# Norm gains on x instead of on w_in and wq, in a two-layer decoder trunk

## The chip, the core and the metric

The kernel runs on one core of one Trainium2 chip. The metric is the device time of one execution in microseconds: the median of several runs. A hardware profile of one such execution shows each instruction of the engines: PE (TensorE, matrix products; its weight loads, PEld, are shown apart), DVE (VectorE), ACT (ScalarE), POOL (GpSimd) and SP, which here issues the loads of weights.

## What is computed

Two layers act on 256 tokens of width 1024, in float32. Each sub-layer normalizes its input first:

```
def rms_norm(x, gain):
    y = x32 * lax.rsqrt(jnp.mean(x32 * x32, axis=-1, keepdims=True) + EPS)
    return (y * gain.astype(jnp.float32)).astype(x.dtype)
...
for l in range(DEPTH):
    h = h + 0.5 * swiglu(rms_norm(h, ffn1_norm[l]), ...)
    h = h + hybrid_mixer(rms_norm(h, mix_norm[l]), w_in[l], ...)
    h = h + memory_cross_attention(rms_norm(h, xattn_norm[l]),
                                   rms_norm(mem, mem_norm[l]), wq, wkv, wo)
    h = h + 0.5 * swiglu(rms_norm(h, ffn2_norm[l]), ...)
return rms_norm(h, final_norm)
```

The mixer multiplies by one matrix `w_in` (1024 x 2048), whose columns give the input of a state-space model and q, k and v of a differential attention. The cross attention's queries are `rms_norm(h) @ wq` (1024 x 1024). A gain has one number per input column, that is, per row of the weight matrix: `(x * gain) @ w` is the same as `x @ (gain * w)`. The factor `rsqrt(...)` is one number per token and is multiplied into the product afterwards.

## The kernel before

**Three products for one.** Operands are split into a high part in the fast float32 format (fp32r) and a low part, the remainder. A product is the sum of three: high x high, high x low, low x high. ACT makes the high part (a copy, `whi` for weights, `xh` for x), DVE the low one (source minus high part, `wlo`, `xl`). Weights move through the array as the streamed operand, 512 columns at a time; x, transposed, is the loaded one.

**Units.** All weights come in an order made out beforehand (`stream_plan`, L112) as 414 units of 128 x 1024, each loaded by one 512 KB DMA from SP's queue into one of four raw buffers. An entry of the plan holds the name, the layer, the number, a kind, the gain and a skew. Kind A (gate and up weights, `w_in`, `wkv`, `wq`) has two row groups of 128 with 512 columns each, kind B one row group with 1024. Kind S belongs to a scheme of seven products instead of eight in the second-form ffns. Skew 4 marks units of which four are used in a row by the first token tile and then again by the second: the first chunk behind a seam and the units of `blocks`. Skew 1 marks the rest. `chunk` (L140) enters the four units that give 512 output columns.

**Splitting.** A unit is split either in halves or whole. `split_unit` (L606) does one half of 512 columns: where the plan names a gain, ACT copies with it as scale and DVE does `raw * gain - high` as one SCALAR_TENSOR_TENSOR; otherwise it is a plain copy and a subtraction. `split_whole` (L549) does all 1024 columns with one instruction on each engine, without a gain. `feed` (L527) decides when: it goes along the plan, a few planner microseconds ahead of the matmuls, and splits whole where the entry is of an ffn and has no gain, or is of kind S. `tick` calls it before each half unit's matmuls; these wait for the end of the split they read.

**Where gains sit.** In the first ffn of layer 0, in `w_in`, `wkv`, `wq` and `w_out` they are multiplied into the weights. For `ffn2` and for `ffn1` of layer 1 they are multiplied into x: `prep` (L799) adds a sub-layer's output to the residual `h`, transposes it on PE in two halves of four 128 x 128 blocks, and calls `split_gain` (L494) or the plain `split` (L490) on each half. `split_gain` uses four ACT copies and four DVE instructions of 128 columns, one for each block, as each block has its own column of gains; the plain one uses one of 512 on each engine. `prep` runs once per token tile at the start of each sub-layer, then starts the sum of squares for `rstd`.

**Order of work.** Everything is put into a fixed order by a planner inside the program: a clock (`Clock`) adds up modelled costs of each instruction, and tasks (generators) for evacuations, attention and the state-space model are resumed when their modelled time comes. So what an instruction is modelled to cost sets where other instructions are put in each engine's queue.

**Around the change.** `mixer` (L1380) makes four chunks of `w_in`, three of `wkv`, then `w_glu` and `w_out`; `cross` makes two chunks of `wq`, one of `wkv`, then `wo`. `project` (L678) runs one chunk into two PSUM tiles `mm`, one for each tile of 128 tokens. There are two such buffers, so that the evacuation of a chunk (`z`, an ACT copy with `rstd` as scale) must be done before the next chunk's matmuls for that tile. The first chunk of a sub-layer runs all of token tile 0, then all of tile 1. In the trace the tile names tell the stage: `mm<-whi,xh` are products of x, `mm<-whi,mem` those of the memory (`wkv`), `acc<-whi,gT` the ffns' down products, `acc<-whi,yT` those of `w_glu`. Most instructions carry the line of a helper: L369 the matmuls, L380 the transposes, L330 ACT, L293 DVE.

Of the kernel before, what the change touches and what calls it, by code (L numbers as in the profile page):

```python
# [76 lines left out]
def second_items(nm):  # L77

    seen = {}
    for item in (SECOND if nm == "ffn2" else SECOND_ONE).split():  # L80
        k = seen[item] = seen.get(item, -1) + 1
        yield item[0], int(item[1:]), k
# [29 lines left out]
def stream_plan():  # L112

    plan = []
    for l in range(L):
        def ffn(nm):
            for j in range(NCH):
                for kp in range(4):
                    plan.append((nm + "_gu", l, 4 * j + kp, "A", (nm, l, 2 * kp), 4 if j == 0 and len(plan) >= 4 else 1))
                if j >= LAG:  # L120
                    for f in range(2):
                        plan.append((nm + "_dn", l, 2 * (j - LAG) + f, "B", None, 1))
            for n in range(2 * (NCH - LAG), 2 * NCH):
                plan.append((nm + "_dn", l, n, "B", None, 2 * LAG))

        def second(nm):
            for kind, j, k in second_items(nm):
                if kind == "P":
                    plan.append((nm + "_gu", l, 4 * j + k, "A", None, 4 if j == 0 else 1))
                elif kind == "D":  # L130
                    plan.append((nm + "_dn", l, 2 * j + k, "B", None, 1))
                else:
                    _, loads, operand, add = PAIR[k]
                    for u in range(2):
                        n = [4 * (j + a) + 2 * b + u for _, a, b in loads]
                        plan.append((nm + "_gu", l, n, "S", ((nm, l, j), u, [x[0] for x in loads], operand, add), 1))
            for n in range(2 * (NCH - LAG), 2 * NCH):
                plan.append((nm + "_dn", l, n, "B", None, 2 * LAG))

        def chunk(nm, c, norm, skew):  # L140
            for kp in range(4):
                plan.append((nm, l, 4 * c + kp, "A", (norm, l, 2 * kp), skew))

        ffn("ffn1") if l == 0 else second("ffn1")
        for c in range(4):
            chunk("w_in", c, "mix", 4 if c == 0 else 1)
        for c in range(3):
            chunk("wkv", c, "mem", 1)
        for k in range(4):
            plan.append(("w_glu", l, k, "B", None, 4))  # L150
        for k in (4, 5, 6, 7, 0, 1, 2, 3):
            plan.append(("w_out", l, k, "B", ("ssm", l, k) if k < 4 else ("sub", l, 0), 4))
        for c in range(2):
            chunk("wq", c, "xattn", 4 if c == 0 else 1)
        chunk("wkv", 3, "mem", 1)
        for k in range(8):
            plan.append(("wo", l, k, "B", None, 4))
        second("ffn2")
    need, at, i = [], 0.0, 0
    while i < len(plan):  # L160
        n = plan[i][5]
        need += [at + STEP * k for k in range(n)]
        at += STEP if plan[i][3] == "S" else 2 * STEP * n
        i += n
    ahead, at, stage = [], 0, None
    for nm, l, n, kind, _, skew in plan:
        at = at + 1 if (nm[:4], l) == stage else 0
        stage = nm[:4], l
        long = nm[:3] == "ffn" and at >= 16 and skew == 1 or nm == "w_in" and at >= 4 or nm == "wkv" and n < 8
        ahead.append(LEAD_LONG if long else LEAD)  # L170
    return plan, need, ahead
# [213 lines left out]
class Trunk:  # L385
    def __init__(self, ctx, tc, io):
# [19 lines left out]
        self.tp = P("tp", 1, space=bass.MemoryType.PSUM)  # L406
        self.dram = P("dram", 1, space=bass.MemoryType.DRAM)
        self.plan, self.need, self.ahead = stream_plan()
        self.main = 0.0
        self.upos = self.nload = self.nsplit = self.nfree = 0  # L410
# [116 lines left out]
    def feed(self, least=-1):  # L527

        c = self.c
        prev, c.cur = c.cur, self.stream  # L530
        n = len(self.plan)
        while self.nsplit < 2 * n:
            u, q = divmod(self.nsplit, 2)
            if u >= self.nfree + N_W or (u > least and self.need[u] + q * STEP / 2 > self.main + self.ahead[u]):
                break
            self.split_next(self.plan[u][0].startswith("ffn") and self.plan[u][4] is None or self.plan[u][3] == "S")
        c.cur = prev

    def split_next(self, whole=False):
# [259 lines left out]
    def prep(self, t, acc, coef, gain=None):  # L799
        h = self.h[t]  # L800
        t0 = []
        for n in range(2):
            s = slice(512 * n, 512 * n + 512)
            self.v.scalar_tensor_tensor(h[:, s], acc[n], coef, h[:, s], op0=ALU.mult, op1=ALU.add)
            t0.append(self.c.cur.t)
        self.acc_done()
        x = self.xt()
        for n in range(2):
            self.c.cur.t = t0[n]
            yield  # L810
            yield from self.tp_wait()
            p = self.transpose4(h, [512 * n + 128 * i for i in range(4)])
            if gain is not None:
                self.split_gain(x, n, p, *gain)
            else:
                o = [a[:, 4 * n:4 * n + 4, :].rearrange("p a b -> p (a b)") for a in x]
                self.split(o[0], o[1], p)
            self.tp_done(p)
        self.x[t] = x
        with self.c.aside():  # L820
            self.row_stat(t)
# [1083 lines left out]
    def run(self):  # L1905
        c = self.c
        self.setup()
        preps = None
        prep = lambda coef, gain=None: (lambda t, acc: self.prep(t, acc, coef, gain))
        z, tb = {}, {}  # L1910
        small = c.spawn(self.ssm_small(z), START[0])
        tables = self.tables(0, z, tb, small)
        c.spawn(self.chain(self.setup_mem(0), self.setup_mem(1), self.setup_bias(), self.setup_lam()), START[1])
        for l in range(L):
            if l == 0:
                preps = self.ffn("ffn1", preps, prep(0.5))
            else:
                tb, tables = {}, []
                preps = self.ffn_second("ffn1", preps, prep(0.5), lambda: tables.extend(self.tables(l, z, tb, None)))
            preps = self.mixer(l, preps, tb, tables, prep(1.0))  # L1920
            preps = self.cross(l, preps, prep(1.0, ("ffn2", l)))
            if l == L - 1:
                self.fn = self.s4t([128, 1024], name="fn")
                self.g.dma_start(self.fn, self.io["final_norm"].to_broadcast([128, 1024]))
            preps = self.ffn_second("ffn2", preps, prep(0.5, ("ffn1", l + 1)) if l < L - 1 else (lambda t, acc: self.final(t, acc, 0.5)))
        c.wait(*preps)
        c.drain()
        assert self.upos == len(self.plan) == self.nfree
# [9 lines left out]
def lay_out(a):  # L1938
# [11 lines left out]
    for l in range(L):  # L1950
# [9 lines left out]
        groups["w_glu", l] = type_b(f["ssm_w_glu"][l])  # L1960
        groups["w_out", l] = type_b(f["w_out"][l])
    wst = np.concatenate([groups[s, l][i:i + 1] for s, l, n, _, _, _ in stream_plan()[0] for i in (n if isinstance(n, list) else [n])], axis=0)
    col = lambda v: v.reshape(-1, 128).T
    gains = np.concatenate(
# [31 lines left out]
```

## Time and profile before

| | us |
|---|---|
| median of 3 runs (1193.57 to 1193.97) | 1193.92 |
| the profiled execution | 1193.89 |
| its span, first to last instruction | 1192.1 |
| DMA traffic read, MB | 207.00 |

The page of the profile gives the busy time of each engine, its share of the span, and the longest groups of instructions. In such a group `whi<-raw,gains 128x512 ... x280 | 184.0, 714 | 10.6` means: written tile, read tiles, shape, count, busy us, mean ns of one, and idle us of the engine just ahead of them with what ended it. In the timeline a row has the start, the length, the engine and the instruction; equal neighbours are merged and counted. Matmuls overlap on PE, so the time that one costs is the distance between two starts, not its length. Idle time of an engine is put down to what it waited for.

The first mixer's products begin at about 208 us of the span and its `w_in` part ends at about 262 us; its cross attention begins at about 346 us, the second ffn of layer 0 at 418 us. Layer 1's mixer begins at about 794 us, its cross attention at 933 us.

### The profile page before, as it was taken

The numbers are of one execution on the slowest core, as the hardware profiler recorded it, in microseconds if no ns is written. First come the engines' busy times: TensorE is split into PE (matmuls) and PEld (weight loads), VectorE is DVE, ScalarE is ACT, GpSimd is POOL, SyncE is SP. The second block draws the span as 40 slices with busy tenths as digits, with TensorE's granted clock in tenths as the row PEclk, the third lists the DMA queues.
The fourth block names the chain that finished last, engine by engine and source line by source line (L and its number), as shares of the span: only waits on it lengthen the run. The fifth ranks groups of instructions, "written<-read, shape, count | busy, mean of one in ns | idle before, by whom it ended". The sixth has DMA issues, their size and how long they took to land.

```text
span 1192.1 us, 17474 instructions
## 1 busy us (share of the span) xinstructions
PE 1182.4 (99%) x6571; PEld 967.8 (81%) x6571; DVE 909.7 (76%) x1331; ACT 707.1 (59%) x1141; POOL 46.7 (4%) x104
## 2 busy tenths in 40 slices
PE   9999999999999999999999999999999999999997
PEld 7888788877888888888888887888778888888886
DVE  5799676598767688889588985766978575888885
ACT  6665554656866566565466644455767665656553
POOL 1200001000100000000000000010001000000000
PEclk9999999999999999999999999999999999999999
DMA  8656545644544465474557364556436445836542
GB/s 276 227 185 208 156 165 170 195 126 140 177 160 141 159 229 213 142 263 126 176 199 266 123 199 150 176 154 180 150 101 208 150 149 176 305 120 240 183 125 87
DMA packets 59973, 210.90 MB, mean 177 GB/s; under 512 B 7168, under 2 KB 8288, under 8 KB 59888
## 3 DMA queue, kind: packets, MB, share of 16 engines
q1 hardware_dynamic: 56304, 202.92, 52.1%
q0 software_dynamic: 2000, 5.24, 1.6%
q10 hardware_dynamic: 1584, 1.62, 0.6%
q8 instruction: 51, 0.84, 0.3%
q14 instruction: 34, 0.28, 0.1%
HBM read 207.00 MB, written 1.05 MB: 175 GB/s over the span
## 4 chain that ended last, share of the span: by engine, by line
PE 97%; ACT 1%; issue 0%; DMA 0%; DVE 0%; POOLq 0%; POOL 0%; ACTq 0%; DVEq 0%
PE mm L369 50%; PE acc L369 33%; PE tp L369 10%; PE tp L380 5%; DMA gains<-in_gains 0%; ACT junk L330 0%; ACT whi L330 0%; DVE h L293 0%; DVE ang L293 0%; ACT on L330 0%; ACT z L330 0%; DVE wlo L293 0%; POOLq L1992 0%; ACT xh L330 0%; POOL rstd L353 0%
## 5 line engine op out<-in xcount | busy, mean ns | idle before, releaser
L369 PE MATMUL mm<-whi,xh 128*128 128x512 f32 x736 | 295.3, 401 | 1.1 <-ACT whi L330 1.0
L293 DVE TENSOR_TENSOR wlo<-raw,whi 128x1024 fp32r<-128x1024 f32 (+1 forms) x228 | 248.0, 1108 | 51.8 <-ACT whi L330 51.1
L369 PE MATMUL mm<-whi,xl 128*128 128x512 f32 x736 | 287.5, 391 | 0.0
L369 PE MATMUL mm<-wlo,xh 128*128 128x512 f32 x736 | 286.9, 390 | 0.3 <-DVE wlo L293 0.3
L330 ACT ACTIVATE whi<-raw 128x1024 fp32r<-128x1024 f32 (+1 forms) x228 | 214.0, 967 | 54.6 <-PE acc L369 25.6
L293 DVE SCALAR_TENSOR_TENSOR wlo<-raw,gains,whi 128x512 fp32r<-128x512 f32 x280 | 198.7, 746 | 53.0 <-ACT whi L330 50.9
L369 PE MATMUL acc<-whi,gT 128*128 128x512 f32 (+1 forms) x704 | 235.3, 395 | 0.0
L330 ACT ACTIVATE whi<-raw,gains 128x512 fp32r<-128x512 f32 x280 | 184.0, 714 | 10.6 <-PE mm L369 4.6
L369 PEld LDWEIGHTS mm<-whi,xh 128*128 128x128 f32 x736 | 138.2, 188 | 31.7 <-ACT whi L330 1.6
L369 PEld LDWEIGHTS mm<-whi,xl 128*128 128x128 f32 x736 | 138.1, 188 | 29.6 <-DVE xl L293 0.3
L369 PEld LDWEIGHTS mm<-wlo,xh 128*128 128x128 f32 x736 | 138.5, 188 | 26.5 <-DVE wlo L293 1.0
L369 PEld LDWEIGHTS acc<-whi,gT 128*128 128x128 f32 x704 | 132.0, 188 | 26.5
L369 PE MATMUL acc<-wlo,gT 128*128 128x512 f32 (+1 forms) x352 | 136.8, 389 | 0.0
L369 PE MATMUL mm<-whi,mem 128*128 128x512 f32 x256 | 92.4, 409 | 0.2
L330 ACT ACTIVATE z<-mm,rstd 128x256 f32<-128x256 f32 (+1 forms) x70 | 37.8, 547 | 71.7 <-PE mm L369 71.1
L369 PEld LDWEIGHTS acc<-wlo,gT 128*128 128x128 f32 x352 | 66.3, 188 | 12.1
L330 ACT ACTIVATE gT<-tp 128x512 fp32r<-128x512 f32 x44 | 26.4, 599 | 60.4 <-PE tp L380 60.3
L369 PEld LDWEIGHTS mm<-whi,mem 128*128 128x128 f32 x256 | 48.1, 188 | 12.7 <-ACT z L330 1.6
L293 DVE TENSOR_TENSOR wlo<-blkX,whi 128x1024 fp32r<-128x1024 f32 x40 | 48.6, 1220 | 9.9 <-ACT whi L330 9.9
L330 ACT ACTIVATE whi<-blkX 128x1024 fp32r<-128x1024 f32 x40 | 42.0, 1055 | 19.5 <-PE mm L369 7.0
L369 PE MATMUL mm<-wlo,mem 128*128 128x512 f32 x128 | 50.2, 393 | 0.0
L293 DVE TENSOR_TENSOR gT<-tp,gT 128x512 fp32r<-128x512 f32 x44 | 30.3, 688 | 24.6 <-ACT gT L330 24.6
(261 smaller groups left out, 1583.4 us busy)
## 6 DMA issues: line engine op xcount, KB each, us to landing
raw<-in_wst SPq DMA_DIRECT2D x342, 512.0 KB, 4.1
blkX<-in_wst SPq DMA_DIRECT2D x10, 512.0 KB, 4.6
blkP<-in_wst SPq DMA_DIRECT2D x10, 512.0 KB, 7.9
blkY<-in_wst SPq DMA_DIRECT2D x10, 512.0 KB, 9.0
blkQ<-in_wst SPq DMA_DIRECT2D x10, 512.0 KB, 9.6
raw<-in_wst SPq DMA_DIRECT2D x4, 256.0 KB, 5.7
mem<-in_mem POOLq DMA_DIRECT2D x2, 512.0 KB, 4.3
uq<-z ACTq DMA_DIRECT2D x8, 128.0 KB, 5.8
```

Source lines behind the costliest of these rows:

```text
L293: r = getattr(self.e, name)(*a, **k)
L330: r = self.e.activation(out, in_, func, **k)
L369: r = self.e.matmul(out, lhsT, rhs, **k)
L380: r = self.e.transpose(out, in_, ident)
```

## The change

Four places of the code differ. The entries of `w_in` and `wq` in the plan lose their gain. The `prep` in front of the mixer and of the cross attention gets it instead, so that these call `split_gain` on x. The test in `feed` now asks for `ffn`, `w_in` or `wq`, without a gain, and for skew 1. Units of the ffns with skew 4 are thereby split in halves too. The number of matmuls, transposes and loads stays as it is.

```
         def chunk(nm, c, norm, skew):
             for kp in range(4):
-                plan.append((nm, l, 4 * c + kp, "A", (norm, l, 2 * kp), skew))
+                plan.append((nm, l, 4 * c + kp, "A", norm and (norm, l, 2 * kp), skew))
...
         for c in range(4):
-            chunk("w_in", c, "mix", 4 if c == 0 else 1)
+            chunk("w_in", c, None, 4 if c == 0 else 1)
...
         for c in range(2):
-            chunk("wq", c, "xattn", 4 if c == 0 else 1)
+            chunk("wq", c, None, 4 if c == 0 else 1)
...
-            self.split_next(self.plan[u][0].startswith("ffn") and self.plan[u][4] is None or self.plan[u][3] == "S")
+            self.split_next(self.plan[u][0][:3] in ("ffn", "w_i", "wq") and self.plan[u][4] is None and self.plan[u][5] == 1 or self.plan[u][3] == "S")
...
             if l == 0:
-                preps = self.ffn("ffn1", preps, prep(0.5))
+                preps = self.ffn("ffn1", preps, prep(0.5, ("mix", l)))
             else:
                 tb, tables = {}, []
-                preps = self.ffn_second("ffn1", preps, prep(0.5), lambda: tables.extend(self.tables(l, z, tb, None)))
-            preps = self.mixer(l, preps, tb, tables, prep(1.0))
+                preps = self.ffn_second("ffn1", preps, prep(0.5, ("mix", l)), lambda: tables.extend(self.tables(l, z, tb, None)))
+            preps = self.mixer(l, preps, tb, tables, prep(1.0, ("xattn", l)))
```

## The prediction

> **What bounds the kernel now.** I read the page first: the span, the busy shares, and the chain that ended last.
>
> ```profile
> span 1192.1 us, 17474 instructions
> ...
> PE 1182.4 (99%) x6571; PEld 967.8 (81%) x6571; DVE 909.7 (76%) x1331; ACT 707.1 (59%) x1141; POOL 46.7 (4%) x104
> ...
> PE 97%; ACT 1%; issue 0%; DMA 0%; DVE 0%; POOLq 0%; POOL 0%; ACTq 0%; DVEq 0%
> ```
>
> The tensor engine covers 99% of the span and 97% of the chain. Busy does not prove that it is at its peak, since its matmuls overlap: one of 512 columns lasts about 0.39 us here, and a wait shorter than that hides inside "busy". So the second view is the chain of waits in order of time, for the rate of a stretch without a break.
>
> ```profile
> 50.34 10.88 PE mm L369 x48
> ```
>
> 48 matmuls in 10.88 us are 0.227 us from one to the next. That is the floor, and the change adds or removes no matmul and no transpose: only time that the engine loses above this floor can move the end. The third view, the engine's timeline, shows such losses. I looked for places where the next matmul starts later than 0.227 us, and for those that only a wait explains. In the first layer's mixer and at the seams around it the plain ones are these (two matmuls merged into one row last 0.61 us when nothing holds them):
>
> ```profile
> 250.21 0.51 PE L369 MATMUL mm<-whi,xh 128*128 128x512 f32 x1
> 250.55 0.40 PE L369 MATMUL mm<-wlo,xh 128*128 128x512 f32 x1
> ...
> 297.32 0.97 PE L369 MATMUL mm<-whi,mem 128*128 128x512 f32 x2
> ...
> 315.00 0.61 PE L369 MATMUL acc<-whi,yT 128*128 128x512 f32 x2
> 315.62 0.50 PE L369 MATMUL acc<-wlo,yT 128*128 128x512 f32 x1
> 315.96 0.63 PE L369 MATMUL acc<-whi,yT 128*128 128x512 f32 x2
> ...
> 728.68 0.39 PE L369 MATMUL acc<-whi,gT 128*128 128x512 f32 x1
> 729.18 0.50 PE L369 MATMUL mm<-whi,xh 128*128 128x512 f32 x1
> ...
> 883.70 0.97 PE L369 MATMUL mm<-whi,mem 128*128 128x512 f32 x2
> ```
>
> At 250.21 the next start comes 0.34 us later, 0.11 too much. At 297.32 the pair takes 0.97 instead of 0.61, so 0.36. At 315.00 two starts take 0.62 instead of 0.45, and the one behind them 0.34, so 0.17 + 0.11. Together 0.75 us in a layer; the second layer repeats them (883.70 is the twin of 297.32), so 1.5 us, and the hole at 728.68, 0.50 - 0.23 = 0.27, makes 1.8 us. **All that the mixers can give back is about 1.8 us of 1192.1, or 0.15%.** A measurement of this kernel can tell about 0.2% (2.4 us) from no change.
>
> **The change part by part.** The weights' copies, and the weight loads, are grouped in the view of instructions by line and shape (busy us, mean ns after the count):
>
> ```profile
> L293 DVE TENSOR_TENSOR wlo<-raw,whi 128x1024 fp32r<-128x1024 f32 x180 | 217.1, 1220 | 38.1 <-ACT whi L330 37.7
> L293 DVE SCALAR_TENSOR_TENSOR wlo<-raw,gains,whi 128x512 fp32r<-128x512 f32 x280 | 198.7, 746 | 53.0 <-ACT whi L330 50.9
> L330 ACT ACTIVATE whi<-raw 128x1024 fp32r<-128x1024 f32 x180 | 186.6, 1057 | 44.5 <-PE acc L369 15.5 <-DMA raw<-in_wst 10.3 <-PE mm L369 7.0
> L330 ACT ACTIVATE whi<-raw,gains 128x512 fp32r<-128x512 f32 x280 | 184.0, 714 | 10.6 <-PE mm L369 4.6 <-issue 2.6 <-DVE wlo L293 1.3
> ...
> L369 PEld LDWEIGHTS mm<-whi,xh 128*128 128x128 f32 x736 | 138.2, 188 | 31.7 <-ACT whi L330 1.6 <-issue 1.3 <-DVE z L293 0.9
> ...
> L293 DVE TENSOR_TENSOR wlo<-raw,whi 128x512 fp32r<-128x512 f32 x48 | 30.9, 687 | 13.7 <-ACT whi L330 13.4
> ...
> L330 ACT ACTIVATE whi<-raw 128x512 fp32r<-128x512 f32 x48 | 27.4, 632 | 10.2 <-PE acc L369 10.2
> ...
> L293 DVE TENSOR_TENSOR xl<-tp,xh 128x512 fp32r<-128x512 f32 x28 | 19.3, 689 | 20.9 <-ACT xh L330 20.9
> ...
> L330 ACT ACTIVATE xh<-tp 128x512 fp32r<-128x512 f32 x28 | 16.7, 597 | 47.2 <-PE tp L380 47.2
> ...
> L330 ACT ACTIVATE xh<-tp,gains 128x128 fp32r<-128x128 f32 x48 | 13.6, 368 | 25.3 <-PE tp L380 25.3
> L293 DVE SCALAR_TENSOR_TENSOR xl<-tp,gains,xh 128x128 fp32r<-128x128 f32 x48 | 13.5, 345 | 5.3 <-ACT xh L330 5.3
> ```
>
> Neighbours on an engine overlap, so I price by busy over count: with a gain and 512 columns 0.657 (ACT) and 0.710 us (DVE); without, 0.571 and 0.644; whole units of 1024, 1.037 and 1.206; for x, a plain 512 costs 0.597 and 0.689, four gained 128s cost 4 x 0.283 = 1.13 and 4 x 0.281 = 1.12.
>
> Removed: w_in has 16 units a layer and wq 8, so 48 units or 96 gained halves: ACT -63.1, DVE -68.2 us. In their place come 32 whole units (those with skew 1): +33.2 and +38.6; and 16 units in plain halves (the first chunk of each, skew 4): +18.3 and +20.6. The streams so get lighter by 11.6 us (ACT) and 9.0 (DVE).
>
> Added: at four stage starts, two token tiles of two halves each, 16 plain copies of x become 64 gained ones: +8.6 on ACT, +7.0 on DVE. And the new condition asks for skew 1 of the ffn units too: the first chunk and the last four down units of the three second-form ffns and the last four of the first ffn, 28 units, fall back from whole to halves: 56 x 0.571 - 28 x 1.037 = +2.9 on ACT, +2.3 on DVE.
>
> **Net: -0.1 us on ACT and +0.3 on DVE.** The change saves next to no engine time; it moves about 10 us per engine from the streams to stage starts and seams. So the question is only whether the matmuls notice at either place.
>
> The streams: a first half of a whole unit now waits until 1024 columns are split. The tightest w_in half before:
>
> ```profile
> 222.66 4.07 DVE L293 SCALAR_TENSOR_TENSOR wlo<-raw,gains,whi 128x512 fp32r<-128x512 f32 x6 [1.84 <-ACT whi L330]
> ```
> ```profile
> 226.01 0.39 PE L369 MATMUL mm<-wlo,xh 128*128 128x512 f32 x1
> ```
>
> The first of these six copies, done about 223.41, is read by the matmul at 226.01: 2.6 us early. A whole unit delays a first half by at most one half copy, 0.6 us, and its second half comes no later. No hole; the cover is that lead. The loads behind it, on SP's queue, start when the raw buffer is released, with the second half as now; queue and sizes stay.
>
> The starts: behind the transposes of the residual, PE's queue needs x, and ACT's and DVE's queues hold the first chunk's weights behind it. Without gains (first mixer) and with them (second ffn) this looks so:
>
> ```profile
> 203.48 0.60 ACT L330 ACTIVATE xh<-tp 128x512 fp32r<-128x512 f32 x1 [6.06 <-PE tp L380]
> 203.97 0.71 ACT L330 ACTIVATE whi<-raw,gains 128x512 fp32r<-128x512 f32 x1
> ```
> ```profile
> 413.88 2.27 ACT L330 ACTIVATE xh<-tp,gains 128x128 fp32r<-128x128 f32 x8 [6.18 <-PE tp L380]
> 416.02 1.07 ACT L330 ACTIVATE junk<-h 128x1024 bf16<-128x1024 f32 x1
> ```
> ```profile
> 210.75 1.40 DVE L293 SCALAR_TENSOR_TENSOR wlo<-raw,gains,whi 128x512 fp32r<-128x512 f32 x2
> ```
> ```profile
> 212.62 0.39 PE L369 MATMUL mm<-wlo,xh 128*128 128x512 f32 x1
> ```
>
> One plain half occupies ACT 0.49 us (203.48 to 203.97), so two 0.98; eight gained copies 2.14 (413.88 to 416.02): +1.16 us per tile ahead of the weights. The tightest weight behind the first tile is the first of the two at 210.75: done about 211.49, read at 212.62, 1.1 us early. From 1.16 I take back what the lighter halves give, 0.09 on ACT (0.657 - 0.571) and 6 x 0.066 on DVE (0.710 - 0.644): net 0.7 later, 0.4 us left. If the give-back fails, 0.05 is missing and the matmul behind it costs 0.11 more: 0.16 at each of four starts, 0.6 us. The second tile's x has a precedent, the ffn's start:
>
> ```profile
> 423.46 2.25 DVE L293 SCALAR_TENSOR_TENSOR xl<-tp,gains,xh 128x128 fp32r<-128x128 f32 x8 [0.60 <-ACT xh L330]
> ```
> ```profile
> 424.36 0.40 PE L369 MATMUL mm<-whi,xl 128*128 128x512 f32 x1
> ```
>
> The first low part is there at 423.81 (0.345 after its start), 0.55 before its matmul, and nothing stops. The sum of squares, and with it POOL's rstd, comes the same 1.16 later for each tile; the evacuations that need it stand behind 24 matmuls (5.4 us). Cost zero, upper end 0.6. The ffn's own start now gets half units, of which the first is ready sooner: zero.
>
> What no row shows is how the planner, whose modelled costs change, regroups the small-matrix bursts among the matmuls:
>
> ```profile
> 233.29 0.69 PE mm L369 x3
> ...
> 235.06 0.89 PE mm L369 x3
> ```
>
> Three matmuls take 0.89 us behind a burst of small matrices and 0.69 otherwise. A burst split off or merged is worth 0.2 us; five either way, my estimate from some twenty such groups in a mixer, make 1.0 us. I take zero, the row as it stands.
>
> Sum: 0 on the profiled execution, whose own time is 1193.89 us (span 1192.1, the rest around it), beside a median of 1193.92. **Forecast 1193.9 us**, with its own range 1192.9 to 1195.5 (1.0 of bursts down; 1.0 and 0.6 of starts up).
>
> **The rivals.**
> (1) Faster: the lighter streams close the holes. 1193.9 - 1.8 = 1192.1; with five bursts merged 1191.1. For it: the hole at 315.00 waits for a low part made late by a full DVE. Against it: it lies in w_glu, far behind w_in, and nothing there gets lighter.
>
> (2) Slower: evacuation behind wide copies. A chunk has two PSUM tiles, and the next chunk's first matmuls write into them, so ACT must evacuate between:
>
> ```profile
> 247.76 0.71 ACT L330 ACTIVATE whi<-raw,gains 128x512 fp32r<-128x512 f32 x1
> ...
> 249.47 0.68 ACT L330 ACTIVATE z<-mm,rstd 128x512 f32<-128x512 f32 x1
> ```
>
> The second evacuation ends at 250.15 and the matmul at 250.21 has waited for it. If a whole copy (1057 ns, not 714) stands in front, it is 0.34 later, plus the 0.11 behind every hole: 0.45. There are four such boundaries per layer in the mixer and two in the cross attention, 12 in all: 5.4 us at most, 2.7 if half are hit, so 1196.6. It decides from the point where a whole copy starts inside the last 0.34 us before an evacuation that has no slack. Against it: here ACT sits idle for 0.50 us between the two, waiting for a transpose, which would swallow the 0.34.
> The Trainium skill speaks for this one ("Perfetto Trace Analysis", Optimizing Scalar/DVE Operations): larger operations help where the engine is saturated, and where it isn't but causes bubbles elsewhere, breaking instructions up may help. By that rule whole units are the wrong way at 59% of ACT; the trace shows one place in reach and decides nothing yet.
>
> (3) PE only looks full, matmuls hide waits for DVE throughout, and lighter streams shorten them by all that DVE is relieved of there: 1193.9 - 9.0 = 1184.9. Against it, the unbroken 0.227 us. The skill's rule ("Perfetto Trace Analysis", Identifying the Most-Contended Engine) is to judge PE by its weight loads' busy share, not by matmuls'; by it the 81% would leave room. Trace: a load lasts 0.188 us of each 0.227, 83%, in stretches without any wait, so 81% is nearly its ceiling here.
>
> (4) The planner puts the copies at the old times and the relief becomes idle time on ACT and DVE: the forecast's time.
>
> **How the numbers follow.** Forecast with (4) 0.70, (1) 0.15, (2) 0.13, (3) 0.02. Faster by over 0.2% (below 1191.5): a quarter of (1) and all of (3), 0.06. Slower by over 0.2% (above 1196.3): two thirds of (2), 0.09. Same: 0.85. The range runs from 1191.9, just past the 1.8 us of holes, to 1196.0, past the forecast's upper end and into (2); it leaves out about 0.15.
>
> **What would show it.** Counts: 184 whole plain weight splits, 136 plain halves, 184 gained ones, 112 gained copies of x. ACT's and DVE's busy sums within about 2 us of 707.1 and 909.7. PE's gaps at 297, 315 and 729 unchanged; a w_in chunk's matmuls free of new holes. Rival (2) would show as later first matmuls of chunks with an evacuation just ended; a start that fails, as a late second matmul in the fourth unit of a first chunk. I am wrong if the span moves by more than 2.4 us, or if the busy sums do not balance.

## The result and the profile after

The changed kernel takes 1216.03 us (median of 5 runs, 1215.08 to 1217.04) beside 1193.92 for the one before (1193.52 to 1194.18) on the same chip: a ratio of 1.0185, 95% interval 1.0174 to 1.0197. That is 22.1 us slower, and outside the range that the prediction gave. Its page has these lines:

```profile
span 1214.2 us, 17567 instructions
...
PE 1188.4 (98%) x6571; PEld 973.1 (80%) x6571; DVE 910.6 (75%) x1375; ACT 708.8 (58%) x1187; POOL 45.4 (4%) x104
...
PEclk9999999999899999999999999999989999999999
...
PE 94%; ACT 3%; DMA 1%; issue 1%; DVE 1%; ACTq 0%; POOLq 0%; POOL 0%; DVEq 0%
```

ACT and DVE do what was forecast: 708.8 and 910.6 us, 1.7 and 0.9 more than before. The number of PE's instructions is the same. Yet PE's share of the chain fell from 97% to 94%, and in two of the 40 slices, one in each layer, the granted clock is below nine tenths. So PE waits somewhere, although ACT and DVE have hardly more to do.

To see where, I cut the span at events that both kernels have: the transposes of `h` with which the mixers, the cross attentions and the second ffn begin. The view of windows gives for each stretch its length, the busy time of PE, PEld, DVE, ACT and POOL, the granted clock and the DMA share. Before:

```profile
202.84:341.52 138.68, 138.59 (x949) 110.41 (x948) 105.44 (x167) 93.30 (x184) 6.60 (x13) 1.00 0.53 160
341.52:413.25 71.73, 71.73 (x386) 61.21 (x385) 46.94 (x83) 44.10 (x83) 1.48 (x4) 1.00 0.47 147
413.25:789.25 376.00, 375.88 (x1925) 308.50 (x1924) 300.04 (x356) 211.31 (x284) 9.67 (x20) 1.00 0.56 187
789.25:927.92 138.67, 138.58 (x949) 110.42 (x948) 105.55 (x167) 93.30 (x184) 6.60 (x13) 1.00 0.54 160
```

After:

```profile
202.54:352.46 149.92, 140.94 (x949) 112.49 (x948) 104.81 (x167) 92.58 (x185) 5.99 (x13) 0.98 0.49 148
352.46:424.21 71.75, 71.75 (x386) 61.08 (x385) 47.37 (x91) 44.09 (x91) 1.48 (x4) 1.00 0.47 147
424.21:800.41 376.20, 376.05 (x1925) 308.69 (x1924) 300.93 (x372) 213.08 (x300) 8.07 (x18) 1.00 0.56 187
800.41:949.68 149.27, 140.96 (x950) 112.54 (x948) 104.80 (x167) 92.54 (x185) 7.55 (x16) 0.97 0.50 150
```

The first column after the window settles it: the mixers take 11.24 and 10.60 us longer (149.92 - 138.68, 149.27 - 138.67), the cross attention 0.02, the ffns 0.2. Together 22.1. DVE and ACT are even less busy in the mixers than before.

The view of waits for PE, here over the whole span, names the place, once in each mixer: line of the waiting instruction, what it waited for, total us, times, longest us.

```profile
PE tp L380 <- DVE yT L293: 15.2, 2, 7.6
PE tp L380 <- ACT up L330: 1.3, 2, 0.9
```

PE's timeline there, in layer 0:

```profile
296.92 1.04 PE L380 MATMUL tp<-ident,yg 128*128 128x128 f32 x8
305.57 1.11 PE L380 MATMUL tp<-ident,z 128*128 128x128 f32 x4 [7.61 <-DVE yT L293]
...
306.90 0.63 PE L369 MATMUL mm<-wlo,mem 128*128 128x512 f32 x1
307.33 1.05 PE L369 MATMUL mm<-whi,mem 128*128 128x512 f32 x2
```

`yg` is the state-space model's output after the Gelu; `ssm_out` (L1494) transposes it in two groups of four blocks, and ACT and DVE split each group into `yT`. Each group fills one of the two transpose buffers `tp` in PSUM (`tpt`, L429), and the buffer is free when DVE has read it. Here both groups stand directly behind each other, so both buffers are taken, and the next thing in PE's queue, the transposes of `z` for the memory's keys, needs a third. Behind them in the queue stand matmuls of `wkv`. PE stands still for 7.61 us. And why does `yT` take so long? ACT's timeline:

```profile
293.74 1.28 ACT L330 ACT_TABLE_LOAD   x1
295.04 1.08 ACT L330 ACTIVATE yg<-acc 128x512 f32<-128x512 f32 x2
...
298.86 0.67 ACT L330 ACTIVATE z<-mm,rmem 128x512 f32<-128x512 f32 x1
299.54 1.28 ACT L330 ACT_TABLE_LOAD   x1
300.83 0.51 ACT L330 ACTIVATE sb<-sb,nm 128x256 f32<-128x256 f32 x1
...
302.81 0.67 ACT L330 ACTIVATE z<-mm,rmem 128x512 f32<-128x512 f32 x1
303.38 1.94 ACT L330 ACTIVATE yT<-tp 128x512 fp32r<-128x512 f32 x2
```

Between the Gelu and `yT` stand a weight copy, a copy `on` and a norm's squares (all in the gap from 296 on), a `z`, a load of the exponential's table and four exponentials of the attention (`sb`). Before, the exponentials were through before the Gelu, one table load fewer lay in between, and the two groups of `yg` came apart, with matmuls in between:

```profile
288.41 0.51 ACT L330 ACTIVATE sb<-sb,nm 128x256 f32<-128x256 f32 x1 [1.38 <-DVE nm L293]
...
298.25 1.28 ACT L330 ACT_TABLE_LOAD   x1
299.55 1.09 ACT L330 ACTIVATE yg<-acc 128x512 f32<-128x512 f32 x2
```
```profile
302.51 0.60 PE L380 MATMUL tp<-ident,yg 128*128 128x128 f32 x4
...
307.28 0.60 PE L380 MATMUL tp<-ident,yg 128*128 128x128 f32 x4
```

Behind the stop PE is slow for a while. In the windows view the clock column reads 0.50:

```profile
305.60:310.00 4.40, 4.40 (x15) 3.71 (x16) 4.26 (x10) 1.21 (x2) 0.00 (x0) 0.50 0.02 4
```

From 306.90 to 307.33 one matmul is 0.43 us from the next, not 0.227. Half a clock for 4.4 us costs 2.2 us. The rest of layer 0 is in the early mixer, where two waits are new:

```profile
221.10 0.50 PE L369 MATMUL mm<-whi,xh 128*128 128x512 f32 x1 [0.21 <-ACT z L330]
...
231.18 1.09 PE L380 MATMUL tp<-ident,up 128*128 128x128 f32 x8 [0.94 <-ACT up L330]
```

So layer 0 reads: 7.6 of stop, 2.2 of half clock, and about 1.6 of early waits (starts 0.60 apart at 220.50 instead of 0.227, the 0.11 behind it, and 1.33 at 229.85 instead of 0.227): 11.4 by this sum, 11.24 measured.

### The profile page after: what moved, and what is told of

Its sections match the earlier page's. It is cut to its first block, busy times and chain, and to the rows that moved or that the text cites. A ratio compares the mean times of both kernels' runs of the same rounds, so it can differ in the third digit from the quotient of the medians.

```text
span 1214.2 us, 17567 instructions
## 1 busy us (share of the span) xinstructions
PE 1188.4 (98%) x6571; PEld 973.1 (80%) x6571; DVE 910.6 (75%) x1375; ACT 708.8 (58%) x1187; POOL 45.4 (4%) x104
## 3 DMA queue, kind: packets, MB, share of 16 engines
q10 hardware_dynamic: 1584, 1.62, 0.5%
## 4 chain that ended last, share of the span: by engine, by line
PE 94%; ACT 3%; DMA 1%; issue 1%; DVE 1%; ACTq 0%; POOLq 0%; POOL 0%; DVEq 0%
PE mm L369 47%; PE acc L369 32%; PE tp L369 10%; PE tp L380 5%; DMA uq<-z 1%; ACT whi L330 1%; ACT junk L330 0%; ACT z L330 0%; ACT L330 0%; PE pz L369 0%; ACT sb L330 0%; ACTq L339 0%; ACT yg L330 0%; DVE yT L293 0%; ACT yT L330 0%
## 5 line engine op out<-in xcount | busy, mean ns | idle before, releaser
L293 DVE TENSOR_TENSOR wlo<-raw,whi 128x1024 fp32r<-128x1024 f32 (+1 forms) x320 | 309.7, 994 | 98.0 <-ACT whi L330 97.1
L330 ACT ACTIVATE whi<-raw 128x1024 fp32r<-128x1024 f32 (+1 forms) x320 | 268.4, 879 | 68.9 <-PE acc L369 24.9
L293 DVE SCALAR_TENSOR_TENSOR wlo<-raw,gains,whi 128x512 fp32r<-128x512 f32 x184 | 130.9, 747 | 19.5 <-ACT whi L330 17.8
L330 ACT ACTIVATE whi<-raw,gains 128x512 fp32r<-128x512 f32 x184 | 120.8, 712 | 0.7 <-DVE wlo L293 0.4
L330 ACT ACTIVATE xh<-tp,gains 128x128 fp32r<-128x128 f32 x112 | 31.9, 377 | 56.5 <-PE tp L380 56.5
```

The source lines that it names most:

```text
L293: r = getattr(self.e, name)(*a, **k)
L330: r = self.e.activation(out, in_, func, **k)
```

## The experiments

The theory to test, called O below: the work of each engine is not what costs, but the order in which the planner writes it, and the whole splits of `w_in` tipped that order. The rivals: G, the gains on x at the stage starts; F, the ffn units that fall back to halves; E, evacuations behind copies of 1024 columns (rival (2) of the prediction); Q, each whole split of `w_in` costs its share. All times are medians; ratios are to the kernel before, run on the same chip.

**1. Whole splits, no gains on x.** The changed plan, with `prep` plain in front of mixer and cross attention. So the `mix` and `xattn` gains are left out altogether. The test in `feed` takes the first ffn units whole again, as before the change:

```
-            self.split_next(self.plan[u][0][:3] in ("ffn", "w_i", "wq") and self.plan[u][4] is None and self.plan[u][5] == 1 or self.plan[u][3] == "S")
+            self.split_next(self.plan[u][4] is None and (self.plan[u][0].startswith("ffn") or self.plan[u][0][:3] in ("w_i", "wq") and self.plan[u][5] == 1) or self.plan[u][3] == "S")
...
-                preps = self.ffn("ffn1", preps, prep(0.5, ("mix", l)))
+                preps = self.ffn("ffn1", preps, prep(0.5))
...
-            preps = self.mixer(l, preps, tb, tables, prep(1.0, ("xattn", l)))
+            preps = self.mixer(l, preps, tb, tables, prep(1.0))
```

> Leaves out the mix and xattn gains altogether; the w_in and wq units of skew 1 are split whole, ffn units as before. Theory O (the whole splits of w_in shift the order in which PE's and ACT's queues are written, and a z transpose of the wkv keys stands behind a tp slot that waits for yT): both 7.8 us holes of PE near 298 and 895 are there, 10 us per layer with the half-rate matmuls behind them, so 20 us slower than before, about 1214. Theory G (the gains on x at the stage starts cost it): no gain is left, so about 1194. Theory F (ffn units back in halves): none is changed here, about 1194. Theory E (evacuations behind 1024-wide copies): twelve boundaries of at most 0.5 us, 1195 to 1200, no hole of 7.8 us.

1212.91 us, ratio 1.0163 (1.0146 to 1.0180). The stop is there, with no gain on x anywhere:

```profile
295.07 1.04 PE L380 MATMUL tp<-ident,yg 128*128 128x128 f32 x8
303.73 1.11 PE L380 MATMUL tp<-ident,z 128*128 128x128 f32 x4 [7.62 <-DVE yT L293]
```

G and F can't make it, since neither is in this kernel, and E allowed no stop of this length. But not all of the loss is there: the two mixers take 148.61 and 147.29 us, 9.93 and 8.62 more than before, and that is 3.3 us less than in the changed kernel. The early waits for `z` and `up` are absent; run 9 comes back to them.

**2. Gains on x, no whole splits.** The changed kernel with the old test in `feed`:

```
-            self.split_next(self.plan[u][0][:3] in ("ffn", "w_i", "wq") and self.plan[u][4] is None and self.plan[u][5] == 1 or self.plan[u][3] == "S")
+            self.split_next(self.plan[u][0].startswith("ffn") and self.plan[u][4] is None or self.plan[u][3] == "S")
```

> The gains of mix and xattn go onto x as in the changed kernel, but the w_in and wq halves stay halves, now plain copies, and the ffn units stay whole as before. Theory O: no hole of 7.8 us, one PE wait of a few tenths per stage start at most, 1193 to 1197. Theory G: most of the 22 us, 1210 or more. Theories E and F: about 1194.

1194.34 us, ratio 1.0006 (0.9997 to 1.0016): no difference that can be told. Its first mixer:

```profile
202.49:341.47 138.98, 138.87 (x950) 110.33 (x948) 105.39 (x179) 92.39 (x196) 6.58 (x13) 1.00 0.53 160
```

138.98 us against 138.68: the gained copies of x, without whole splits, cost at most 0.3 us per mixer. G alone falls.

**3. The ffn units in halves, alone**, as `... and self.plan[u][4] is None and self.plan[u][5] == 1 ...` for the ffns in the kernel before.

> Before, with the first ffn units of a stage (skew above 1) back in halves as in the changed kernel; nothing else. Theories O, G and E: 28 units cost 2.9 us of ACT and 2.3 us of DVE, hidden, 1193 to 1195. Theory F: part of the 22 us, above 1198.

1194.37 us, ratio 1.0005 (0.9996 to 1.0015). F falls as well.

**4. The cross attention's half of the change alone**: gains of `xattn` on x, `wq` whole, all else as before.

> The change for the cross attention's queries alone: xattn gains on x, wq units of skew 1 split whole; w_in and the ffn units as before. Theory O: w_in is untouched, so the order in the mixer is that of before, 1193 to 1196. Theory G: a third to a half of the loss, 1201 to 1205.

1193.64 us, ratio 1.0000 (0.9991 to 1.0009). So the loss needs the whole splits of `w_in`. Whether by their amount (Q) or by the order they lead to, the next pair tells.

**5 and 6. The same work, two orders.** `w_in`'s first chunk (units 0 to 3) is in halves anyway. Of the other three, two are left whole and one goes back to plain halves: the fourth in run 5, the second in run 6.

```
-... and self.plan[u][5] == 1 or self.plan[u][3] == "S")
+... and self.plan[u][5] == 1 and (self.plan[u][0] != "w_in" or self.plan[u][2] < 12) or self.plan[u][3] == "S")
```

Run 6 has `>= 8` in place of `< 12`. The counts of split instructions are equal: 1383 instructions on DVE in both.

> The changed kernel with the w_in units of the fourth column chunk back in plain halves: 8 whole w_in units a layer where the change has 12. In its program the eight yg transposes still stand together and the z transposes right behind them. Theory O (order): the two 7.8 us holes stay, 1210 to 1217. Rival Q (each whole w_in split costs a share of the 22 us): two thirds of it, about 1208.

> The changed kernel with the w_in units of the second column chunk back in plain halves: 8 whole w_in units a layer too, the same work for ACT and DVE to the instruction as with the fourth chunk in halves. In its program the eight yg transposes come as two fours with wkv matmuls between, the z transposes before them, and the exponentials ahead of the Gelu. Theory O: no hole of 7.8 us, 1193 to 1199. Rival Q: two thirds of the loss, about 1208.

Fourth chunk in halves: 1217.13 us, ratio 1.0192 (1.0175 to 1.0209). Second chunk in halves: 1195.57 us, ratio 1.0014 (1.0004 to 1.0023). The first still has its stop, in both layers:

```profile
PE tp L380 <- DVE yT L293: 15.3, 2, 7.6
```

In the second, the two groups of `yg` stand apart, `z` comes ahead of them, and no wait for `yT` is left; from its timeline:

```profile
300.73 0.60 PE L380 MATMUL tp<-ident,z 128*128 128x128 f32 x4
...
303.26 0.60 PE L380 MATMUL tp<-ident,yg 128*128 128x128 f32 x4
```

Equal work, 21.6 us apart. Q would have put both at 1208, so the amount of whole splits does not set the loss. The orders differ, but so does the place of the whole units; run 11 changes the order alone.

**7. One rule to mend the order.** In the changed kernel the Gelu waits, in the planner, until all four groups of exponentials of the layer have been written:

```
+            while st.get("exps", 0) < 4:
+                yield c.now + 0.3
             yg = self.s4t([128, 4, 8, 2, 16], name="yg")
...
+                st["exps"] = st.get("exps", 0) + 1
```

> The changed kernel with one wait more in the order's planner: the Gelu of the SSM output is written only after all four groups of exponentials of the layer's attention. Every split as in the changed kernel. Theory O: the exponentials and the second table load no longer stand between yg and yT, the z transposes come ahead of the yg transposes, the 7.8 us holes go; one or two shorter holes may come where PE waits for what is late instead, 1194 to 1203; ACT's table loads back from 13 to 11. Rivals that put the loss on the splits or the gains themselves: 1212 or more still.

1210.18 us, ratio 1.0136 (1.0121 to 1.0151): a miss of my expectation by 7 us. The wait for `yT` is gone and the table loads are back to 11, but two other places are now late. A `z` evacuation has come behind the exponentials:

```profile
298.20 0.66 PE L380 MATMUL tp<-ident,z 128*128 128x128 f32 x4 [2.29 <-ACT z L330]
```

and in `w_out`, where the low parts of the weights are late, PE stops again:

```profile
334.31 0.50 PE L369 MATMUL acc<-wlo,xh 128*128 128x512 f32 x1 [1.35 <-DVE wlo L293]
```

What I took for the defect, exponentials between Gelu and `yT`, was one of several things in the wrong place. Moving it moved the stop.

**8. Only PE's order mended.** In the changed kernel the `z` transposes of the keys' second chunk wait, in the planner, until the `yT` splits have been written (`for x in after + [ys] * ch`). ACT's order there stays.

> The changed kernel with the z transposes of the keys' second chunk held, in the written order, until the yT splits are written; ACT's order is unchanged. If the tp slot behind which the z transposes stood is the whole of the stall, the holes go and the time is about 1196. If ACT's order is the root (exponentials and z behind them in front of yT), PE runs on until the next wkv product lacks an mm bank, whose z copy is the one at 302.81: 297.7 to 303.5 less two halves of 0.68, holes of about 4.4 us a layer in place of 7.8, so 1207 to 1211.

1212.18 us, ratio 1.0150 (1.0135 to 1.0166). The stop breaks up as the second alternative had it:

```profile
297.59 1.04 PE L380 MATMUL tp<-ident,yg 128*128 128x128 f32 x8
300.25 0.50 PE L369 MATMUL mm<-whi,mem 128*128 128x512 f32 x1 [1.62 <-ACT z L330]
...
304.21 0.75 PE L369 MATMUL mm<-whi,mem 128*128 128x512 f32 x1 [2.31 <-ACT z L330]
```

The two waits are 3.9 us long together, where 4.4 was expected by starts. The total came out 1 us above the range given: the half clock still follows, and lasts longer than the 4.4 us behind the single stop, from 304.2 to 311.0, as the windows' clock column shows (third from the end):

```profile
304.20:306.20 2.00, 1.61 (x3) 0.79 (x3) 1.05 (x2) 2.00 (x3) 0.00 (x0) 0.52 0.00 0
...
308.00:311.00 3.00, 3.00 (x9) 2.43 (x9) 2.89 (x7) 1.85 (x4) 0.00 (x0) 0.50 0.02 5
```

So both orders have a share, though mending PE's alone gave back only about 4 of the 22 us: PE's queue put a buffer's next user right behind the two groups that fill both buffers, and ACT's queue, with exponentials and a table load, held back `yT` and the `z` evacuations alike.

**9. One chunk whole.** Only the second chunk of `w_in` whole, to size the early waits.

```
+... and (self.plan[u][0] != "w_in" or self.plan[u][2] < 8) ...
```

> The changed kernel with only the second column chunk's w_in units whole (4 a layer), chunks three and four back in plain halves. Its written order around yg is that of before: yg transposes in two fours, z ahead of them. It keeps what the changed kernel does at chunk one to two. Theory O: no 7.8 us hole; the early-mixer waits near 220, 230 and 818, 828 (z and the uq and up copies behind 1024-wide whi copies) stay, 2.5 us in layer 0 and 1.9 in layer 1, so 1196 to 1200. If those early waits are themselves a product of the later order, 1194 to 1196.

1196.59 us, ratio 1.0022 (1.0013 to 1.0031). Both early waits are there without the late stop, the second of them so:

```profile
230.81 0.88 PE L380 MATMUL tp<-ident,up 128*128 128x128 f32 x6 [0.56 <-ACT up L330]
```

The first, for `z`, is mechanism E. ACT's timeline of the changed kernel shows it:

```profile
218.47 2.01 ACT L330 ACTIVATE whi<-raw 128x1024 fp32r<-128x1024 f32 x2 [1.45 <-PE mm L369]
220.38 0.67 ACT L330 ACTIVATE z<-mm,rstd 128x512 f32<-128x512 f32 x1
```

Before, this `z` began at 219.93; now two wide copies hold it until 220.38. But the wide copies do not do it alone. Run 1 has the same two in front of the same `z`, without gains on x, and there they end before the `z` could start, which waits for its own matmul:

```profile
219.75 0.69 ACT L330 ACTIVATE z<-mm,rstd 128x512 f32<-128x512 f32 x1 [0.23 <-PE mm L369]
```

With the gains on x, ACT begins the `z` of the first token tile, ahead of the wide copies, 0.92 us later (216.29 in the changed kernel and 216.31 in run 2, 215.37 in run 1), and so the copies too (218.47, 217.51). So at this boundary E needs both the wide copies and the gains on x. The second early wait is for `up`, a copy that needs the DMA `uq<-z` issued right after that `z`; it too is absent in run 1. E is real, but PE waits for it at one chunk boundary of a mixer, and it costs a share of 1.2 us per mixer (140.00 and 139.78 us against 138.7).

**10. Run 6 with the ffns' first units whole again**, as a version that might beat both kernels.

> The version with chunks three and four whole (1195.57), with the first ffn units of a stage whole again as in before. It has the change's relief on ACT and DVE at two thirds and none of its holes. Since PE bounds the kernel, 1193.5 to 1195.5; faster than before only if some of the 1.8 us of small holes close, which nothing in the trace of the version with halved ffn units shows.

1194.76 us, ratio 1.0007 (0.9998 to 1.0017). It beats the changed kernel by 21 us and not the one before.

**11. The order alone.** The kernel before, every split as it was. In the planner alone, one group of softmax transposes is held back by 6 us:

```
+                if t and not hp:
+                    yield c.now + 6.0
                 yield from self.tp_wait()
```

> Before, with every split, gain and weight as it was; in the written order alone, the softmax transposes of the second query tile's first head pair are held back by 6 us of the planner's clock. Its program then has the exponentials and Gelu next to each other and the eight yg transposes together. If the order alone, without any change of a split, costs PE holes, 1197 to 1208; if the loss needs whole splits, 1194.

1208.06 us, ratio 1.0118 (1.0103 to 1.0133): 14 us lost without a change of any split, a hair above the range given. The `yg` groups came together here too, and this time it is the transposes of the attention's output `on` that need the third buffer:

```profile
303.30 1.03 PE L380 MATMUL tp<-ident,yg 128*128 128x128 f32 x8
...
308.92 1.12 PE L380 MATMUL tp<-ident,on 128*128 128x128 f32 x4 [3.89 <-DVE yT L293]
```

The stop is half as long. ACT has made its part of `yT` by 306.1 here (two copies from 304.09, 2.01 us in all); it is DVE that comes to it late, behind the softmax's instructions:

```profile
307.81 2.04 DVE L293 TENSOR_TENSOR yT<-tp,yT 128x512 fp32r<-128x512 f32 x2
```

The two mixers take 145.11 and 145.33 us, 6.4 and 6.7 more than before. What the two orders have in common is that both `tp` buffers are filled by `yg` and a third user stands close behind in PE's queue. Which one it is, and what delays `yT`, differs.

**12. What there was to gain.** The kernel before with the `mix` and `xattn` gains left out altogether, halves kept.

> Before, with the mix and xattn gains left out altogether: the w_in and wq halves stay halves but become plain copies and subtractions, nothing is added to x. Its written order is that of before. It shows what the relief of ACT and DVE in the streams could be worth at most with the order held. If PE alone bounds the kernel, 1193.4 to 1194.3; if ACT or DVE still set the pace anywhere in these streams, 1192.9 or less.

1193.81 us, ratio 1.0000 (0.9991 to 1.0010). ACT falls to 698.9 and DVE to 903.8 us of busy time, 8.2 and 5.9 less than before, and nothing comes of it.

## Why the prediction was wrong, step by step

**Right.** PE bounds the kernel, and there was nothing to win: run 12 takes 8.2 us from ACT for nothing. Rivals (1) and (3), which saw a gain in lighter streams, are out with it. The four counts came exactly; the view of groups of the changed kernel, by shape:

```profile
L293 DVE TENSOR_TENSOR wlo<-raw,whi 128x1024 fp32r<-128x1024 f32 x184 | 222.7, 1222 | 70.3 <-ACT whi L330 69.8
...
L330 ACT ACTIVATE whi<-raw,gains 128x512 fp32r<-128x512 f32 x184 | 120.8, 712 | 0.7 <-DVE wlo L293 0.4 <-DMA gains<-in_gains 0.3
...
L330 ACT ACTIVATE whi<-raw 128x512 fp32r<-128x512 f32 x136 | 76.9, 640 | 17.1 <-PE acc L369 15.3 <-DVE wlo L293 1.4 <-DMA raw<-in_wst 0.3
...
L330 ACT ACTIVATE xh<-tp,gains 128x128 fp32r<-128x128 f32 x112 | 31.9, 377 | 56.5 <-PE tp L380 56.5
```

The engine sums moved by +1.7 and +0.9 where -0.1 and +0.3 were given, inside the 2 us allowed; ACT's sum contains two more table loads of 1.28 us each, which come from the order and not from the splits. The step on the starts holds when taken alone: in run 2 at most 0.3 us in each of two mixers and nothing in the cross attentions, just under the upper end of 0.6 for four starts. The step on the 28 ffn units holds (run 3).

**Wrong: the step "What no row shows is how the planner, whose modelled costs change, regroups the small-matrix bursts among the matmuls".** It priced a change of order at 0.2 us for each burst split off or merged, five either way, and took zero, "the row as it stands". That row shows what a moved burst costs PE in itself. What a moved instruction costs through a resource was left out: it can take a buffer that a later one needs, and every instruction behind the waiting one in PE's queue waits too. That is not 0.2 us but as long as the slowest chain that frees the buffer, here 7.6 us, with 2.2 us lost to the half clock after it, in each layer. So the zero stood beside an upper end that was far too low, and the trace of before had rows for a better one: the two `yg` groups stand 4.8 us apart (302.51 and 307.28) with matmuls between, ACT's share of one `yT` takes 1.1 us, and a table load with a Gelu 2.4 us of ACT (298.25 to 300.64). A stop of several us in each layer was within reach if those groups moved together.

A smaller gap lies in the same sum: the starts and the streams were priced apart, at zero each. Alone each is near that (run 2; no early wait in run 1). Together they make the early waits, and the mixers of the changed kernel are 1.3 and 2.0 us longer than those of run 1.

**Rival (2), slower, had the right sign and a true mechanism at a wrong size.** Of the four boundaries in a mixer PE waited at one, at 220.50, for 0.37 + 0.11 us, near the 0.45 that the rival gave to each; it hit fewer than half, and only with x's gains in front, which the rival did not name. Its 1196.6 is what run 9 gave (1196.59), but that agreement is luck: there it is partly the `up` wait, which the rival did not name either. The rule of the Trainium skill that the prediction set beside it ("Perfetto Trace Analysis", Optimizing Scalar/DVE Operations) points the right way there: whole units cost where ACT was not saturated. Run 6, with two of three chunks whole and 1.7 us lost, says that this share is small. By run 10 some 0.8 of the 1.7 would be the ffns' first units, but the intervals of the two ratios overlap.

**Rival (4)** forecast no loss, since the planner would put the copies where they were. It did not.

**What stays open.** Why the planner wrote this order for some sets of whole chunks and not for others wasn't settled. The code has one place that could do it: in `Clock.pe` (L273) a task whose modelled time lies ahead pulls the whole clock forward (`self.now = max(self.now, t.t + 0.13)`), and in `ssm_out` the second group's transposes carry the modelled end of the first group's split. That was only read, not tried. Of the `up` wait in layer 0, the rows give the later `z` a small part: its DMAs are issued 0.43 us later than before (221.08, 220.65), yet `up` begins 3.36 us later (230.07, 226.71), and the slowest `uq<-z` takes 8.3 us from issue to landing, where before it took at most 5.4. Why that transfer lands later stays open.

## What to carry to other kernels

Where a program writes its own instruction order from modelled costs, a change of tile size can also be a change of order, and here a forecast that priced only the work left out the larger risk. Before such a change, list the places where a queue meets a small pool of buffers (here two for transposes), and price each by the longest chain that frees one. To test order against work, look for two variants with equal instruction counts and different order, as runs 5 and 6, and for one that changes nothing but the order, as run 11: these three numbers settle what sums of durations could not.

## What the hardware showed unexpectedly

Here a stop of PE costs more than its length, and a short one was enough. After 7.61 us of standing still the granted clock is 0.50 for 4.4 us, as the window above shows. But in run 7 a stop of 2.29 us (298.20) is already followed by half clock; the windows behind it, with the clock in the third number from the end:

```profile
298.10:300.00 1.90, 1.80 (x8) 1.57 (x9) 0.00 (x0) 1.90 (x9) 0.85 (x1) 0.73 0.00 0
300.00:302.00 2.00, 2.00 (x6) 1.46 (x6) 0.00 (x0) 1.97 (x5) 0.00 (x0) 0.50 0.03 8
```

The Trainium skill ("TensorE: Matmul & The Clock Gate", HAM oscillation — how this bites in real kernels) advises against gaps of PE above some 3.4 us. The halving agrees with what that page says of the two states; the length does not, since 2.29 us was enough here. The stop of 1.35 us at 334.31 in the same kernel left the clock alone:

```profile
334.30:337.00 2.70, 2.69 (x14) 2.20 (x15) 1.76 (x4) 0.78 (x2) 0.39 (x1) 1.00 0.82 232
```

So did run 8's first stop of 1.62 us, where the column reads 1.00 from 300 to 302. Whether the length alone decides between these cases, no run here shows.
